# Where tiles begin in the on-chip memory: a pool for small scratch tiles, and other start addresses for weight halves and activations

## The chip, the cores and the metric

The kernel runs on one core of a Trainium2 chip. The core has five engines that run side by side: TensorE (PE in the rows, its weight loads PEld), VectorE (DVE), ScalarE (ACT), GpSimd (POOL) and SyncE (SP), which here issues DMAs. Tiles that the engines read lie in the on-chip memory SBUF, which has 128 partitions; a tile has the same start address, in bytes, on every partition. Matrix products land in another memory, PSUM. The metric is the device time of one execution in microseconds.

## What is computed

Two transformer blocks of depth one run one after the other on 256 tokens of width 2048, all in float32.

```python
# block 1
h = rmsnorm(x, norm_mix_g);  proj = h @ w_in           # 2048 -> 7568 columns
o_a = mla_branch(...);       o_b = dsa_branch(...)     # two kinds of attention
merged = gate0 * (o_a @ w_branch_a) + gate1 * (o_b @ w_branch_b)
x = x + merged @ w_out
x = x + peer_ffn(rmsnorm(x, norm_ffn_g), ...)          # 16384 experts, below
x = rmsnorm(x, norm_final_g)
# block 2: the same frame with an mLSTM and an S5 scan as mixers, then a peer layer and a norm

def peer(x, wq, subkeys, u_tab, v_tab):                # in both blocks
    s = scores(x @ wq, subkeys)                        # two lists of 128 keys per head
    idx, gate = top 16 of the 16 x 16 sums, softmax    # 8 heads x 16 experts per token
    act = gelu(x . u_tab[idx])
    return sum over the 128 chosen of (gate * act) * v_tab[idx]
```

## The kernel before

**Dense experts.** The kernel doesn't gather experts. In each `peer` call it multiplies all 256 tokens with the whole of `u_tab` and, with gates that are zero for experts not chosen, with the whole of `v_tab`. So nearly all of its time goes into matrix products of 256 tokens with weight tiles that come from device memory, 1 MB (128 partitions x 2048 float32) at a time.

**Split operands.** Every such product is made of three matmuls in the format float32r. `weights_now` loads a tile as two halves `w_raw` of 4096 bytes per partition, makes `w_hi` from each on ScalarE (line 198) and `w_lo` = `w_raw` - `w_hi` on VectorE (line 204) or, in part, on GpSimd (line 202). Activations are split in the same way (`split`, lines 252 and 253). `products` (its matmul call is line 213) then issues w_hi x h_hi and w_hi x h_lo in turns, and after them w_lo x h_hi. A matmul has a stationary operand, which is loaded into the array (the LDWEIGHTS rows, 128 columns), and a moving operand, which is streamed through it.

**Three uses of `products`** carry the prediction's steps.

- *u products* (`cols` in `peer`, `in_t`, `gate`, `in_cols`): 128 columns of a weight half are stationary, and 256 columns of `hT_hi` or `hT_lo`, the transposed activations, are moving. PSUM tile `ps_u`. A weight tile makes 48 such matmuls.
- *v products* (`tile_v` in `peer`): 128 columns of the gated activations `coef_hi` or `coef_lo` are stationary, and 512 columns of a weight half are moving. PSUM tile `ps_v`. A weight tile makes 24.
- *row products* (`row_products`, in `rows`, `out_proj`, `lead_products` and for `in2_v`): 128 columns of `hT` are stationary, and 256 to 512 columns of a weight half are moving.

The small ones are those of `mix1` with `cqT`, with `ckvT` and with `o_hi`/`o_lo`, which stand where `hT` stands above.

**Order.** A scheduler of the tile framework sets each engine's order when the program is built. Work for the other engines (routing, gates, attention, scans) is written as generators that `K.step` moves on between weight tiles. Each engine runs its list in order, and semaphores join the lists. The order of `peer` is: queries and routing, then for each half r of the experts one sweep of u products (64 tiles) and one of v products (64 tiles).

**Pools.** A pool is a stretch of SBUF addresses, in which tiles of one tag take turns in `bufs` places. Pools opened on the left stand one behind the other from low addresses, and those with `side="right"` from high ones. Before, the left has const (with `ident`), state (`x` and its squares), weights (`wp`: `w_raw`, `w_hi`, `w_lo`, the `big` tiles, the tags `two_a` and `two_b`, and tiles of a few bytes such as `ss`, `rs_m`, `rs`), and then the pool of the stage at hand; the right has only `top` with `hT`. `two_a` and `two_b` hold `coef_hi` and `coef_lo` among others. Every place is a multiple of 32 bytes.

Of the kernel before, what the change touches and what calls it, by code (L numbers as in the profile page):

```python
# [12 lines left out]
P = 128  # L13
T = 256
TB = 2
# [18 lines left out]
class Ctx:  # L34


    def __init__(self, ctx, tc):
        self.tc, self.nc = tc, tc.nc
        nc = self.nc
        pool = lambda name, bufs, **kw: ctx.enter_context(tc.tile_pool(name=name, bufs=bufs, **kw))  # L40
        self.const = pool("const", 1)
        self.state = pool("state", 1)
        self.top = pool("hT", 1, side="right")
        self.wp = pool("weights", 2)
        self.ps = pool("psum", 2, space=bass.MemoryType.PSUM)
        it = self.const.tile([P, P], F32, name="iota_f")
        nc.gpsimd.iota(it, pattern=[[1, P]], base=0, channel_multiplier=-1,
                       allow_small_or_imprecise_dtypes=True)
        self.diff = it
        self.ident = self.const.tile([P, P], F32, name="ident")  # L50
        nc.vector.tensor_scalar(self.ident, it, 0.0, None, op0=OP.is_equal)
        self.iota = self.const.tile([P, P], F16, name="iota_h")
        nc.gpsimd.iota(self.iota, pattern=[[1, P]], base=0, channel_multiplier=0,
                       allow_small_or_imprecise_dtypes=True)
        self.half_pi = self.const.tile([P, 1], F32, name="half_pi")
        nc.vector.memset(self.half_pi, float(np.pi / 2))
        self.x = self.state.tile([P, TB, D], F32, name="x")
        self.sq = self.state.tile([P, TB, 4], F32, name="x_sq")
        self.sq2 = self.state.tile([P, TB, 4], F32, name="x_sq2")
        self.twice, self.first, self.normed, self.done, self.fused = False, {}, {}, set(), {}  # L60
        self.bg = []
        self.late = []
        self.credit = 0.0
        self.fine = 0
        self.last = None
# [25 lines left out]
            self.square(xx, self.sq[:, tb, c:c + 1])  # L91

    def sum_sq(self, tb, sq):
        ss = self.wp.tile([P, 1], F32, name="ss", bufs=4)
        self.nc.vector.tensor_reduce(ss, sq[:, tb], AX.X, OP.add)
        return ss

# [17 lines left out]
    def norm_begin(self, tb):  # L115

        v = self.nc.vector  # L120
        ss = self.sum_sq(tb, self.sq)
        if self.twice:
            s2 = self.sum_sq(tb, self.sq2)
            e = self.wp.tile([P, 1], F32, name="rs_e", bufs=2)
            v.tensor_scalar(e, ss, EPS / D, EPS * EPS, op0=OP.mult, op1=OP.add)
            rs = self.rsqrt(s2, 1.0 / D, e)
            self.first[tb] = ss
        else:
            rs = self.rsqrt(ss, 1.0 / D)
        for c in range(4):  # L130
            cc = slice(c * 512, (c + 1) * 512)
            n = self.normed_cols(tb, c)
            if (tb, c) in self.fused:
                v.scalar_tensor_tensor(n, self.x[:, tb, cc], rs, self.fused.pop((tb, c)), op0=OP.mult, op1=OP.mult)
            elif (tb, c) not in self.done:
                v.tensor_scalar(n, self.x[:, tb, cc], rs, None, op0=OP.mult)
            elif c % 2:
                self.nc.scalar.activation(n, n, AF.Copy, scale=rs)
            else:
                v.tensor_scalar(n, n, rs, None, op0=OP.mult)  # L140
            self.done.discard((tb, c))
# [95 lines left out]
    def lead_cols(self, src, hh, hl, dst):  # L237

        tiles = [self.weights(src[i], pool=(2048, 1024)[i]) for i in range(2)]
        ps = [self.ps.tile([P, T], F32, name="ps_u", bufs=2) for _ in range(TB)]  # L240
        self.lead_products(ps, tiles, hh, hl, 8, T)
        pt = self.ps.tile([P, 2, T], F32, name="ps_g", bufs=2)
        for tb in range(TB):
            r = self.wp.tile([P, T], F32, name="lead", tag="two_a", bufs=2)
            self.nc.scalar.copy(r, ps[tb])
            for i in range(2):
                self.nc.tensor.transpose(pt[:, i, tb * P:(tb + 1) * P], r[:, i * P:(i + 1) * P], self.ident)
        for i in range(2):
            dst(i, pt[:, i])
# [5 lines left out]
    def rstd(self, src, n, name):  # L255

        nc = self.nc
        junk = self.ps.tile([P, 512], F32, name="ps_u", bufs=2)
        ss = self.wp.tile([P, 1], F32, name=name, tag="rs", bufs=2)
        nc.scalar.activation(junk[:, :n], src, AF.Square, accum_out=ss)  # L260
        return self.rsqrt(ss, 1.0 / n)

    def rsqrt(self, ss, scale, eps=EPS):


        v = self.nc.vector
        m, q, r = (self.wp.tile([P, 1], F32, name=nm, bufs=3) for nm in ("rs_m", "rs_q", "rs_r"))
        v.tensor_scalar(m, ss, scale, eps, op0=OP.mult, op1=OP.add)
        v.tensor_scalar(q.bitcast(I32), m.bitcast(I32), 1, None, op0=OP.logical_shift_right)
        v.tensor_scalar(r.bitcast(I32), q.bitcast(I32), -1.0, float(0x5f3759df), op0=OP.mult, op1=OP.add)  # L270
        v.tensor_scalar(m, m, -0.5, None, op0=OP.mult)
        for _ in range(3):
            v.scalar_tensor_tensor(q, r, m, r, op0=OP.mult, op1=OP.mult)  # L273
            self.last = v.scalar_tensor_tensor(r, q, 1.5, r, op0=OP.add, op1=OP.mult)  # L274
        return r
# [45 lines left out]
def peer(K, wq, keys, u, v, g_out, g_next=None, dst=None, later=None):  # L321
# [8 lines left out]
    nc, ctx = K.nc, ExitStack()  # L330
# [68 lines left out]
    def routing(tb):  # L399
# [23 lines left out]
        nc.vector.tensor_tensor(dif, tv, tv[:, :, 0:1].to_broadcast([P, NH, SEL]), op=OP.subtract)  # L423
        nc.scalar.activation(dif, dif, AF.Exp)
        p_, m1, ms, m3 = new("pos"), new("m1"), new("ms"), new("m3")
        pu, su, au = tv.bitcast(U32), ti, new("au", U32)
        v = nc.vector
        v.tensor_copy(p_, ti)
        v.tensor_scalar(m1, p_, 16.0, None, op0=OP.is_ge)
# [48 lines left out]
    def gates(r, on_pool):  # L478

        def prepare(t0):  # L480
            oh1 = K.wp.tile([P, TG, P], F16, name="oh1", tag="two_a", bufs=2)
            for t in range(TG):
                e = nc.gpsimd if t < on_pool else nc.vector
                e.tensor_scalar(oh1[:, t], K.iota, i1T[:, t0 + t:t0 + t + 1], None, op0=OP.is_equal)  # L484
# [43 lines left out]
    for r in range(2):  # L528
# [29 lines left out]
        for dh in range(2):  # L558
            acc = [[K.ps.tile([P, 512], F32, name="ps_v", bufs=4) for _ in range(2)] for _ in range(TB)]

            def tile_v(jp):
                a = st["A"][jp // 8][:, (2 * jp) % 16:(2 * jp) % 16 + 2]
                ch = K.wp.tile([P, 2, T], F32R, name="coef_hi", tag="two_a", bufs=2)
                cl = K.wp.tile([P, 2, T], F32R, name="coef_lo", tag="two_b", bufs=2)
                K.split(ch, cl, a)
                wh, wl = K.weights(v[dh, r * NJ // 2 + jp])

# [108 lines left out]
def mix1(K, I):  # L676
# [41 lines left out]
    NF = 33  # L718
    inv = wt([NF, 1], "inv", 1)
    nc.gpsimd.dma_start(inv, I["rope_inv"])  # L720
    posi = K.wp.tile([NF, T], I32, name="posi", tag="two_a", bufs=2)
    pap = I["positions"]
    nc.gpsimd.dma_start(posi, bass.AP(tensor=pap.tensor, offset=pap.offset, ap=[[0, NF], [1, T]]))
    gq = K.wp.tile([P, 512], F32, name="gq", tag="two_b", bufs=2)
    nc.gpsimd.dma_start(gq, bass.AP(tensor=I["mla_q_norm_g"].tensor, offset=I["mla_q_norm_g"].offset, ap=[[0, P], [1, 512]]))
    gkv = K.wp.tile([P, 256], F32, name="gkv", tag="two_b", bufs=2)
    nc.gpsimd.dma_start(gkv, bass.AP(tensor=I["mla_kv_norm_g"].tensor, offset=I["mla_kv_norm_g"].offset, ap=[[0, P], [1, 256]]))

    fsel = K.wp.tile([NF, 2, 3, P], F32, name="rope_sel", tag="big", bufs=2)
# [42 lines left out]
    def norm_rows(ps, n, g, dst):  # L772
        nk = n // P
        nms = []
        for tb in range(TB):
            r = K.rstd(ps[tb][:, :n], n, "rs")
            nm = K.wp.tile([P, 512], F32, name="normed", tag="two_a", bufs=2)[:, :n]
            nc.vector.scalar_tensor_tensor(nm, ps[tb][:, :n], r, g, op0=OP.mult, op1=OP.mult)
            nms.append(nm)

# [9 lines left out]
    def rope(dst, ps, kinds):  # L790


        raw = K.wp.tile([P, T], F32, name="rope_raw", tag="two_a", bufs=2)
        nc.scalar.copy(raw, ps)
        m = wt([P, T], "rope_m", 3, tag="one")
        n = 64 if kinds == (1,) else P
# [34 lines left out]
        K.flush()  # L831
        return ps

    both = K.wp.tile([P, T], F32, name="k_both", tag="two_a", bufs=2)
    rope(both, in_t(0), (0, 2))
    for dst, src in ((kpe, 0), (kix, 64)):
        for i in range(2):
# [31 lines left out]
    def attention(dst, scores, V, scale, bias):  # L869

        for hp in range(4):
            pT = wt([P, 2, TB, T], "probsT", 1, tag="four")
            for tb in range(TB):
# [2 lines left out]
                for h in range(2):  # L876
                    scores(S[:, h, :n], 2 * hp + h, tb, n)
                yield 1
                e = K.wp.tile([P, 2, T], F32, name="probs", tag="two_b", bufs=2)
                if bias is None:  # L880
                    m64 = S[:, :, n - 64:n]
                    nc.vector.tensor_tensor(m64, m64, mask[:, 0, None, 64:P].to_broadcast([P, 2, 64]), op=OP.add)
# [321 lines left out]
def mix2(K, I, dram):  # L1204
# [55 lines left out]
    def s5_in(b):  # L1260
# [9 lines left out]
        m1, m2 = wt([P, 2, T], "m1", 2), wt([P, 2, T], "m2", 2)  # L1270
        v.tensor_tensor(m1, px, cb, op=OP.mult)
        v.tensor_tensor(m2, px, sb, op=OP.mult)
        X[b] = xt = K.wp.tile([P, 2, T], F32, name="s5_xt", tag="two_a", bufs=2)
        v.tensor_tensor(xt[:, 0], m1[:, 0], m2[:, 1], op=OP.add)
        v.tensor_tensor(xt[:, 1], m2[:, 0], m1[:, 1], op=OP.subtract)

    def s5_scan(b):
# [4 lines left out]
        for part in range(2):  # L1282
            v.tensor_tensor_scan(st[:, part], mb, xt[:, part], 0.0, op0=OP.mult, op1=OP.add)  # L1283
        m3 = wt([P, 2, T], "m2", 2)
        m4 = K.wp.tile([P, 2, T], F32, name="s5_m4", tag="two_a", bufs=2)
        g.tensor_tensor(m3, st, cb, op=OP.mult)
        v.tensor_tensor(m4, st, sb, op=OP.mult)
        S[b] = m3, m4
# [1 line left out]
    def s5_out(b):  # L1290
        i, q = divmod(b, 4)
        rows = slice(32 * q, 32 * q + 32)
        m3, m4 = S.pop(b)
        s = K.wp.tile([P, 2, T], F32, name="s5_s", tag="two_b", bufs=2)
        g.tensor_tensor(s[:, 0], m3[:, 0], m4[:, 1], op=OP.add)
        g.tensor_tensor(s[:, 1], m3[:, 1], m4[:, 0], op=OP.subtract)
        if q == 0:
            Y[i] = ps_v([P, T])
        return lambda: s5_y(b, s)
# [425 lines left out]
```

## Time and profile before

| | before |
|---|---|
| median of 2 runs | 4360.38 us (4359.77 to 4360.98) |
| the profiled execution, device time | 4360.12 us |
| its span, first to last instruction | 4358.3 us |
| TensorE busy | 4204.3 us, 96% of the span |
| VectorE, ScalarE, GpSimd busy | 3010.1, 2017.6, 1703.3 us |
| TensorE clock granted, mean | 0.987 of the full 2.4 GHz |
| read from device memory | 749.66 MB, 175 GB/s with writes |

The span is the time from the first to the last instruction in the trace; the device time of the same execution is 1.8 us longer. A busy TensorE is one with at least one matmul under way. Matmuls overlap, so the length of one (0.28 us or 0.39 us in the rows) is longer than the distance from its start to the next one's start. The pace of the engine is that distance, and it is read from the start times of the timeline: last start minus first start, divided by the number of matmuls between.

### The profile page before, as it was taken

To read this page: it belongs to the slowest core of one execution; us is meant where nothing else is said; L and a number is where in the kernel's file an instruction comes from. 1 tells how busy PE (TensorE), PEld (TensorE's weight loads), DVE (VectorE), ACT (ScalarE), POOL (GpSimd) and SP (SyncE) were. 2 spreads that over 40 slices of the span, in tenths; PEclk is the share of its full clock that TensorE was granted. 3 is DMA by queue.
4 is the path that set the end of the run, shared out by engine and by line. 5 is a ranking of instruction groups with operands and counts; after the bars stand their busy time and mean duration, and the time that the engine had idled before them with its cause. 6 is when DMAs were issued, how large, how long until landed. Compare 5 with 4: busy or idle time off the path is not lost. (4 is left out here: it accounts for less than half of the span.)

```text
span 4358.3 us, 74041 instructions
## 1 busy us (share of the span) xinstructions
PE 4204.3 (96%) x28929; PEld 3811.5 (87%) x28929; DVE 3010.1 (69%) x4756; ACT 2017.6 (46%) x2847; POOL 1703.3 (39%) x1425
## 2 busy tenths in 40 slices
PE   8999999899999999999988889989999999999999
PEld 7999988899877899988877688989998889999887
DVE  7775569987698566655569976897855555665555
ACT  5565444344444444445543365434444444444454
POOL 1100023886396277500126861368800006771000
PEclk9999999999999999999999999999999999999999
DMA  5445554455666555555656545535555555555554
GB/s 176 159 154 185 184 180 136 141 175 171 208 217 208 184 175 175 175 188 189 205 181 184 160 133 173 166 131 180 172 177 191 186 189 179 175 174 179 189 195 163
DMA packets 220465, 769.19 MB, mean 176 GB/s; under 512 B 25200, under 2 KB 31376, under 8 KB 219217
## 3 DMA queue, kind: packets, MB, share of 16 engines
q1 hardware_dynamic: 214978, 744.79, 51.5%
q0 software_dynamic: 5136, 19.67, 1.2%
q8 instruction: 227, 3.72, 0.3%
q14 instruction: 124, 1.02, 0.1%
HBM read 749.66 MB, written 14.70 MB: 175 GB/s over the span
## 5 line engine op out<-in xcount | busy, mean ns | idle before, releaser
L204 DVE TENSOR_TENSOR w_lo<-w_raw,w_hi 128x1024 fp32r<-128x1024 f32 (+3 forms) x1347 | 1691.4, 1289 | 1175.8 <-issue 918.0
L198 ACT CAST w_hi<-w_raw 128x1024 fp32r<-128x1024 f32 (+1 forms) x1388 | 1445.8, 1045 | 1660.7 <-PE ps_v L213 640.8
L213 PE MATMUL ps_u<-hT_hi,w_hi 128*128 128x256 f32 x5712 | 1419.0, 288 | 16.9 <-DVE gate L1385 10.0
L213 PE MATMUL ps_u<-hT_lo,w_hi 128*128 128x256 f32 x5712 | 1404.5, 285 | 0.0
L484 POOL TENSOR_SCALAR oh<-iota_h,i1T 128x128 f16<-128x128 f16 x896 | 918.3, 1042 | 751.8 <-PE ps_v L213 539.6
L213 PEld LDWEIGHTS ps_u<-hT_hi,w_hi 128*128 128x128 f32 x5712 | 1104.9, 193 | 24.2 <-DVE gate L1385 10.3
L213 PEld LDWEIGHTS ps_u<-hT_lo,w_hi 128*128 128x128 f32 x5712 | 1105.1, 193 | 4.5 <-issue 2.9
L213 PE MATMUL ps_u<-hT_hi,w_lo 128*128 128x256 f32 x5712 | 758.1, 285 | 34.2 <-POOL w_lo L202 18.5
L213 PEld LDWEIGHTS ps_u<-hT_hi,w_lo 128*128 128x128 f32 x5712 | 718.4, 193 | 41.2 <-POOL w_lo L202 19.6
L213 PE MATMUL ps_v<-w_hi,coef_lo 128*128 128x512 f32 x2048 | 698.6, 396 | 6.9 <-DVE coef_lo L253 6.9
L213 PE MATMUL ps_v<-w_hi,coef_hi 128*128 128x512 f32 x2048 | 692.7, 395 | 2.1 <-DVE x L89 2.1
L213 PE MATMUL ps_v<-w_lo,coef_hi 128*128 128x512 f32 x2048 | 525.7, 395 | 0.0
L213 PEld LDWEIGHTS ps_v<-w_hi,coef_lo 128*128 128x128 f32 x2048 | 383.3, 188 | 105.4 <-DVE coef_lo L253 13.3
L213 PEld LDWEIGHTS ps_v<-w_hi,coef_hi 128*128 128x128 f32 x2048 | 384.4, 188 | 96.1 <-ACT coef_hi L252 2.5
L213 PEld LDWEIGHTS ps_v<-w_lo,coef_hi 128*128 128x128 f32 x2048 | 384.4, 188 | 92.6
L202 POOL TENSOR_TENSOR w_lo<-w_raw,w_hi 128x768 fp32r<-128x768 f32 (+3 forms) x159 | 320.9, 2024 | 288.5 <-ACT w_hi L198 132.8
L252 ACT CAST coef_hi<-acts 128x512 fp32r<-128x512 f32 x256 | 158.7, 622 | 189.4 <-PE ps_v L213 186.9
L253 DVE TENSOR_TENSOR coef_lo<-acts,coef_hi 128x512 fp32r<-128x512 f32 x256 | 199.5, 780 | 1.1 <-ACT coef_hi L252 1.0
L112 POOL TENSOR_TENSOR normed<-x,gain 128x512 f32<-128x512 f32 x22 | 37.1, 1709 | 368.2 <-DVE x L89 278.1
L213 PE MATMUL ps_v<-w_hi,hT_hi 128*128 128x512 f32 (+2 forms) x288 | 103.7, 369 | 1.5 <-ACT hT_hi L252 1.5
L213 PE MATMUL ps_v<-w_hi,hT_lo 128*128 128x512 f32 (+2 forms) x288 | 103.3, 367 | 0.7 <-DVE hT_lo L253 0.7
L101 POOL DMA_DIRECT2D gain<-in_final_g x1 | 0.6, 593 | 259.9 <-DVE coef_lo L253 259.9
(469 smaller groups left out, 3785.2 us busy)
## 6 DMA issues: line engine op xcount, KB each, us to landing
w_raw<-in_p_u SPq DMA_DIRECT2D x512, 512.0 KB, 3.9
w_raw<-in_p_v SPq DMA_DIRECT2D x512, 512.0 KB, 3.9
w_raw<-in_in_gates SPq DMA_DIRECT2D x64, 512.0 KB, 4.0
w_raw<-in_w_out SPq DMA_DIRECT2D x64, 512.0 KB, 3.7
w_raw<-in_p_q SPq DMA_DIRECT2D x48, 512.0 KB, 3.8
w_raw<-in_in_t SPq DMA_DIRECT2D x38, 512.0 KB, 4.1
w_raw<-in_w_ab SPq DMA_DIRECT2D x32, 512.0 KB, 4.0
w_raw<-in_in_qk SPq DMA_DIRECT2D x32, 512.0 KB, 3.7
```

Of the source, the lines that this page charges most:

```text
L101: self.nc.gpsimd.dma_start(gb, bass.AP(tensor=g.tensor, offset=g.offset, ap=[[0, P], [1, D]]))
L112: eng.tensor_tensor(self.normed_cols(tb, c), self.x[:, tb, cc], gb[:, cc], op=OP.mult)
L198: nc.scalar.copy(hi[i], raw[i])
L202: nc.gpsimd.tensor_tensor(lo[i][:, m:], raw[i][:, m:], hi[i][:, m:].bitcast(F32), op=OP.subtract)
L204: nc.vector.tensor_tensor(lo[i][:, :m], raw[i][:, :m], hi[i][:, :m].bitcast(F32), op=OP.subtract)
L213: self.last_mm = self.nc.tensor.matmul(out, lhsT=a, rhs=b, start=start, stop=stop)
L252: self.nc.scalar.copy(hi, src)
L253: return self.nc.vector.tensor_tensor(lo, src, hi.bitcast(F32), op=OP.subtract)
L484: e.tensor_scalar(oh1[:, t], K.iota, i1T[:, t0 + t:t0 + t + 1], None, op0=OP.is_equal)
```

## The change

The change moves tiles to other addresses. It opens a pool `small` ahead of `state` for the tiles of a few bytes per partition (`x_sq`, `x_sq2`, `ss`, `rs_e`, `rs`, `rs_m`, `rs_q`, `rs_r`), and a pool `two` behind `weights` for the tags `two_a` and `two_b`. It opens `pad3` on the right outside `hT`, with a tile of 448 bytes that is set to zero once on GpSimd at the start; a second pad has size 0 and no tile. In the routing, `au` no longer has a tile and uses the place of `ms`, which makes 512 bytes of room.

```diff
         self.const = pool("const", 1)
+        self.small = pool("small", 1)
         self.state = pool("state", 1)
+        self.wp = pool("weights", 2)
+        self.pad = pool("pad", 1)
+        self.two = pool("pairs", 2)
+        self.pad3 = pool("pad3", 1, side="right")
         self.top = pool("hT", 1, side="right")
-        self.wp = pool("weights", 2)
+        for p, n in ((self.pad, 0), (self.pad3, 448)):
+            if n:
+                nc.gpsimd.memset(p.tile([P, n // 4], F32, name="pad"), 0.0)
...
-        self.sq = self.state.tile([P, TB, 4], F32, name="x_sq")
+        self.sq = self.small.tile([P, TB, 4], F32, name="x_sq")
...
-        ss = self.wp.tile([P, 1], F32, name="ss", bufs=4)
+        ss = self.small.tile([P, 1], F32, name="ss", bufs=4)
...
-        pu, su, au = tv.bitcast(U32), ti, new("au", U32)
+        pu, su, au = tv.bitcast(U32), ti, ms.bitcast(U32)
...
-                ch = K.wp.tile([P, 2, T], F32R, name="coef_hi", tag="two_a", bufs=2)
-                cl = K.wp.tile([P, 2, T], F32R, name="coef_lo", tag="two_b", bufs=2)
+                ch = K.two.tile([P, 2, T], F32R, name="coef_hi", tag="two_a", bufs=2)
+                cl = K.two.tile([P, 2, T], F32R, name="coef_lo", tag="two_b", bufs=2)
```

The other lines of the diff put the remaining tiles of these names into `small` and `two` in the same way. In the two built programs the instructions of TensorE, ScalarE and SyncE stand in the same order with the same semaphore waits; those of VectorE too, but for the name `ms` in the place of `au`; GpSimd has one more, the zeroing of the pad. What differs is where operands begin. In bytes past a multiple of 512:

| tile | before | after |
|---|---|---|
| `w_raw`, `w_hi`, `w_lo` (every half) | 480 | 0 |
| `coef_hi`, `coef_lo` | 384 | 0 |
| `hT_hi`, `hT_lo` | 480 | 32 |
| `cqT`, `o_hi`, `o_lo` | 0 | 0 |
| `ckvT` | 32 | 32 |
| `k_nope`, `q_nope` | 0 | 0 |
| `kpe` | 160 | 160 |
| `q_pe` | 480 | 0 |

Columns that a matmul takes from these tiles start at further multiples of 512 bytes, but for the 344 and 272 column rows.

On GpSimd the start of the program reads, before:

```order
L1721 UNCONDITIONAL_BRANCH
L47 ISA
L47 IOTA iota_f 128x128
L53 IOTA iota_h 128x128
L720 DMA inv<-in_rope_inv 33x1
```

and after:

```order
L1728 UNCONDITIONAL_BRANCH
L51 MEMSET pad 128x112
L54 ISA
L54 IOTA iota_f 128x128
L60 IOTA iota_h 128x128
L727 DMA inv<-in_rope_inv 33x1
```

The zeroing of the pad stands ahead of the two tables, and nothing else has moved.

## Rows read from the trace of the kernel before

**Rows 1.** The page: engine, busy us (share) xinstructions; granted clock in 40 slices.

```profile
PE 4204.3 (96%) x28929; PEld 3811.5 (87%) x28929; DVE 3010.1 (69%) x4756; ACT 2017.6 (46%) x2847; POOL 1703.3 (39%) x1425
...
PEclk9999999999999999999999999999999999999999
```

**Rows 2.** The page's costliest groups: one of three u groups, of three v groups.

```profile
L213 PE MATMUL ps_u<-hT_hi,w_hi 128*128 128x256 f32 x5712 | 1419.0, 288 | 16.9 <-DVE gate L1385 10.0
...
L213 PE MATMUL ps_v<-w_hi,coef_lo 128*128 128x512 f32 x2048 | 698.6, 396 | 6.9 <-DVE coef_lo L253 6.9
```

**Rows 3.** Timeline of PE, u products: start us, length us, instruction, count.

```profile
1499.79 0.28 PE L213 MATMUL ps_u<-hT_lo,w_hi 128*128 128x256 f32 x1
...
1503.51 2.08 PE L213 MATMUL ps_u<-hT_hi,w_lo 128*128 128x256 f32 x16
```

**Rows 4.** Timeline of PE, v products; eight matmuls from the first row to the second.

```profile
1327.09 0.39 PE L213 MATMUL ps_v<-w_hi,coef_hi 128*128 128x512 f32 x1
...
1328.96 2.02 PE L213 MATMUL ps_v<-w_lo,coef_hi 128*128 128x512 f32 x8
1330.82 1.10 PE L213 MATMUL ps_v<-w_hi,coef_hi 128*128 128x512 f32 x4
```

**Rows 5.** Timeline of PE, row products of out_proj; 24 matmuls between these starts.

```profile
561.27 0.39 PE L213 MATMUL ps_v<-w_hi,hT_hi 128*128 128x512 f32 x1
...
566.71 0.39 PE L213 MATMUL ps_v<-w_hi,hT_hi 128*128 128x512 f32 x1
```

**Rows 6.** Timeline of PE, products with cqT moving; 36 matmuls between these starts.

```profile
90.88 1.10 PE L213 MATMUL ps_u<-cqT,w_hi 128*128 128x256 f32 x8
...
95.12 1.10 PE L213 MATMUL ps_u<-cqT,w_hi 128*128 128x256 f32 x8
```

**Rows 7.** Timeline of PE, products with o_hi moving, and what follows them.

```profile
373.30 1.10 PE L213 MATMUL ps_v<-o_hi,w_lo 128*128 128x256 f32 x8
374.24 0.28 PE L213 MATMUL ps_u<-hT_hi,w_hi 128*128 128x256 f32 x1
```

**Rows 8.** Timeline of PE, ckvT stationary (six matmuls), then ckvT moving (six).

```profile
104.02 0.63 PE L213 MATMUL ps_v<-w_hi,ckvT 128*128 128x512 f32 x2
...
105.42 0.63 PE L213 MATMUL ps_v<-w_hi,ckvT 128*128 128x512 f32 x2
...
106.12 0.63 PE L213 MATMUL ps_u<-ckvT,w_hi 128*128 128x256 f32 x4
...
106.83 0.63 PE L213 MATMUL ps_u<-ckvT,w_hi 128*128 128x256 f32 x4
```

**Rows 9.** Timeline of PE, attention scores in plain float32; four records between.

```profile
209.17 0.60 PE L917 MATMUL ps_v<-k_nope,q_nope 128*128 128x256 f32 x2
209.60 0.59 PE L918 MATMUL ps_v<-kpe,q_pe 128*128 128x256 f32 x2
210.04 0.59 PE L917 MATMUL ps_v<-k_nope,q_nope 128*128 128x256 f32 x2
```

**Rows 10.** Windows: stretch, us, busy us (count) by engine, granted clock, DMA share, GB/s.

```profile
700.00:1100.00 400.00, 372.00 (x3354) 366.76 (x3354) 344.81 (x754) 162.96 (x260) 279.56 (x224) 0.97 0.47 158
1120.00:1480.00 360.00, 350.97 (x1497) 277.97 (x1495) 288.71 (x228) 169.16 (x189) 201.34 (x176) 1.00 0.64 209
1500.00:1870.00 370.00, 370.00 (x3452) 368.62 (x3451) 229.17 (x318) 161.41 (x265) 242.86 (x240) 1.00 0.51 174
3250.00:3600.00 350.00, 350.00 (x1501) 281.56 (x1501) 188.73 (x192) 168.56 (x186) 1.96 (x2) 1.00 0.56 187
```

**Rows 11.** Waits of PE: who waited for whom, us in total, times, longest.

```profile
PE ps_u L213 <- DVE w_lo L204: 18.8, 14, 3.3
...
PE ps_v L213 <- DVE coef_lo L253: 6.9, 14, 0.5
```

**Rows 12.** Timeline of the program's start: GpSimd's first table, and its reader.

```profile
0.83 0.23 POOL L47 IOTA iota_f<- 128x128 f32 x1 [0.40 <-POOLq L1718]
...
2.56 0.15 DVE L51 TENSOR_SCALAR ident<-iota_f 128x128 f32<-128x128 f32 x1
```

More of the change, by code (lines that the diff above doesn't have):

```diff
@@ L57, in __init__ @@
         self.x = self.state.tile([P, TB, D], F32, name="x")
-        self.sq = self.state.tile([P, TB, 4], F32, name="x_sq")
-        self.sq2 = self.state.tile([P, TB, 4], F32, name="x_sq2")
+        self.sq = self.small.tile([P, TB, 4], F32, name="x_sq")
+        self.sq2 = self.small.tile([P, TB, 4], F32, name="x_sq2")
         self.twice, self.first, self.normed, self.done, self.fused = False, {}, {}, set(), {}
@@ L123, in norm_begin @@
             s2 = self.sum_sq(tb, self.sq2)
-            e = self.wp.tile([P, 1], F32, name="rs_e", bufs=2)
+            e = self.small.tile([P, 1], F32, name="rs_e", bufs=2)
             v.tensor_scalar(e, ss, EPS / D, EPS * EPS, op0=OP.mult, op1=OP.add)
@@ L243, in lead_cols @@
         for tb in range(TB):
-            r = self.wp.tile([P, T], F32, name="lead", tag="two_a", bufs=2)
+            r = self.two.tile([P, T], F32, name="lead", tag="two_a", bufs=2)
             self.nc.scalar.copy(r, ps[tb])
@@ L258, in rstd @@
         junk = self.ps.tile([P, 512], F32, name="ps_u", bufs=2)
-        ss = self.wp.tile([P, 1], F32, name=name, tag="rs", bufs=2)
+        ss = self.small.tile([P, 1], F32, name=name, tag="rs", bufs=2)
         nc.scalar.activation(junk[:, :n], src, AF.Square, accum_out=ss)
@@ L266, in rsqrt @@
         v = self.nc.vector
-        m, q, r = (self.wp.tile([P, 1], F32, name=nm, bufs=3) for nm in ("rs_m", "rs_q", "rs_r"))
+        m, q, r = (self.small.tile([P, 1], F32, name=nm, bufs=3) for nm in ("rs_m", "rs_q", "rs_r"))
         v.tensor_scalar(m, ss, scale, eps, op0=OP.mult, op1=OP.add)
@@ L480, in prepare @@
         def prepare(t0):
-            oh1 = K.wp.tile([P, TG, P], F16, name="oh1", tag="two_a", bufs=2)
+            oh1 = K.two.tile([P, TG, P], F16, name="oh1", tag="two_a", bufs=2)
             for t in range(TG):
@@ L720, in mix1 @@
     nc.gpsimd.dma_start(inv, I["rope_inv"])
-    posi = K.wp.tile([NF, T], I32, name="posi", tag="two_a", bufs=2)
+    posi = K.two.tile([NF, T], I32, name="posi", tag="two_a", bufs=2)
     pap = I["positions"]
     nc.gpsimd.dma_start(posi, bass.AP(tensor=pap.tensor, offset=pap.offset, ap=[[0, NF], [1, T]]))
-    gq = K.wp.tile([P, 512], F32, name="gq", tag="two_b", bufs=2)
+    gq = K.two.tile([P, 512], F32, name="gq", tag="two_b", bufs=2)
     nc.gpsimd.dma_start(gq, bass.AP(tensor=I["mla_q_norm_g"].tensor, offset=I["mla_q_norm_g"].offset, ap=[[0, P], [1, 512]]))
-    gkv = K.wp.tile([P, 256], F32, name="gkv", tag="two_b", bufs=2)
+    gkv = K.two.tile([P, 256], F32, name="gkv", tag="two_b", bufs=2)
     nc.gpsimd.dma_start(gkv, bass.AP(tensor=I["mla_kv_norm_g"].tensor, offset=I["mla_kv_norm_g"].offset, ap=[[0, P], [1, 256]]))
@@ L776, in norm_rows @@
             r = K.rstd(ps[tb][:, :n], n, "rs")
-            nm = K.wp.tile([P, 512], F32, name="normed", tag="two_a", bufs=2)[:, :n]
+            nm = K.two.tile([P, 512], F32, name="normed", tag="two_a", bufs=2)[:, :n]
             nc.vector.scalar_tensor_tensor(nm, ps[tb][:, :n], r, g, op0=OP.mult, op1=OP.mult)
@@ L790, in rope @@
     def rope(dst, ps, kinds):
-        raw = K.wp.tile([P, T], F32, name="rope_raw", tag="two_a", bufs=2)
+        raw = K.two.tile([P, T], F32, name="rope_raw", tag="two_a", bufs=2)
         nc.scalar.copy(raw, ps)
@@ L832, in in_t @@
         return ps
-    both = K.wp.tile([P, T], F32, name="k_both", tag="two_a", bufs=2)
+    both = K.two.tile([P, T], F32, name="k_both", tag="two_a", bufs=2)
     rope(both, in_t(0), (0, 2))
@@ L878, in attention @@
                 yield 1
-                e = K.wp.tile([P, 2, T], F32, name="probs", tag="two_b", bufs=2)
+                e = K.two.tile([P, 2, T], F32, name="probs", tag="two_b", bufs=2)
                 if bias is None:
@@ L1272, in s5_in @@
         v.tensor_tensor(m2, px, sb, op=OP.mult)
-        X[b] = xt = K.wp.tile([P, 2, T], F32, name="s5_xt", tag="two_a", bufs=2)
+        X[b] = xt = K.two.tile([P, 2, T], F32, name="s5_xt", tag="two_a", bufs=2)
         v.tensor_tensor(xt[:, 0], m1[:, 0], m2[:, 1], op=OP.add)
@@ L1284, in s5_scan @@
         m3 = wt([P, 2, T], "m2", 2)
-        m4 = K.wp.tile([P, 2, T], F32, name="s5_m4", tag="two_a", bufs=2)
+        m4 = K.two.tile([P, 2, T], F32, name="s5_m4", tag="two_a", bufs=2)
         g.tensor_tensor(m3, st, cb, op=OP.mult)
@@ L1293, in s5_out @@
         m3, m4 = S.pop(b)
-        s = K.wp.tile([P, 2, T], F32, name="s5_s", tag="two_b", bufs=2)
+        s = K.two.tile([P, 2, T], F32, name="s5_s", tag="two_b", bufs=2)
         g.tensor_tensor(s[:, 0], m3[:, 0], m4[:, 1], op=OP.add)
```

## Prediction

> **What bounds the kernel now.** I read the page from the top. TensorE is busy for 4204.3 us of the 4358.3 us span, the next engine, VectorE, for 3010.1 us, and TensorE's granted clock stands at the upper of its two levels, 2.4 GHz, in every slice [rows 1]. The costliest groups are the matmuls of line 213 [rows 2]: three u groups of 5712 (17136 matmuls of 256 columns) and three v groups of 2048 (6144 of 512 columns). In the second half of the sweeps TensorE never idles: 370.00 of 370 us and 350.00 of 350 us [rows 10]. There the end is set by nothing but the pace at which matmuls follow each other, so the question is whether start addresses change this pace.
>
> The pace is read from start times. In the u products 31 matmuls take 1503.51 - 1499.79 = 3.72 us, 120.0 ns each [rows 3]. In the v products 16 take 1330.82 - 1327.09 = 3.73 us, 233.1 ns each [rows 4]. Row products of the same 512 columns take 5.44 us for 24, 226.7 ns each [rows 5]. So 256 more columns cost 226.7 - 120.0 = 106.7 ns, which is one column per tick of 2.4 GHz, and every matmul has a rest beyond its columns: 120.0 - 106.7 = 13.3 ns in u, 226.7 - 213.3 = 13.4 ns in row products, 19.8 ns in v. Times their counts, the rests of u and v are 228 us and 122 us: 350 us is the most that better addresses could give.
>
> The rest isn't constant, and the rows differ in where operands start. In brackets is the distance from the stationary operand's start to the moving one's, modulo 512 bytes, from the table of the section on the change.
>
> - u, moving 480, stationary 480 (0): 120.0 ns.
> - `cqT`, moving 0, stationary 480 (32): 36 in 4.24 us, 117.8 ns [rows 6]; `o_hi`, also 0 and 480 (32): 8 in 0.94 us, 117.5 ns [rows 7].
> - `ckvT`, moving 32, stationary 480 (64): 6 in 0.71 us, 118 ns [rows 8].
> - row products, moving 480, stationary 480 (0): 226.7 ns.
> - v, moving 480, stationary 384 (96): 233.1 ns.
> - `ckvT` stationary at 32, moving 480 (-64): 6 in 1.40 us, 233.3 ns [rows 8].
>
> The same shape costs 2.4 ns or 6.5 ns more or less, at the same clock, with the start as the one difference that I can name.
>
> **The change part by part.** The rows of order say that no instruction moves and no wait is added, so no queue gets longer. Three edits cost nothing. The zeroing of the pad is one GpSimd instruction ahead of a table of 0.23 us, which VectorE reads 1.5 us after it is done [rows 12]; without that slack it would cost about 0.2 us. The shared place of `ms` and `au` is written and read by VectorE alone, in the old order with the old waits. The pools of small tiles change only where a few bytes lie.
>
> *u products, 17136.* After the change the moving operand starts 32 bytes past the stationary one (32 and 0). That distance is the one of `cqT` and `o_hi` before (0 and 480). I take their 117.6 ns: 17136 x 2.4 = 41 us less. From below the bound is a matmul that shows hardly any rest: the attention scores in plain float32, which start at 0 and 0 for half of their records, take 0.87 us for four records, 217.5 ns each [rows 9]; that is twice the 106.7 ns of 256 columns, 213.3 ns, and a rest of 4.2 ns. With it a u matmul would take 110.9 ns, 156 us less in sum. From above: with a moving start of 480, a stationary start of 384 or 32 costs 6.5 ns more than one of 480, and 0 is one more that isn't 480; 17136 x 6.5 = 111 us more.
>
> *v products, 6144.* Moving and stationary start at 0 and 0. The distance 0 has the row products' 226.7 ns as its nearest row, and the start 0 and 0 has the scores' 217.5 ns for as long a stream, in another format. I take the middle, 222 ns: 6144 x 11.1 = 68 us less. The bounds are 217.5 ns (96 us less) and 233.1 ns (no gain). More than 233.1 ns I exclude, since it is the highest pace for 512 columns in the rows.
>
> *Row products with `hT` stationary,* 864 of 512 columns and some 670 shorter. The distance goes from 0 to -32, between 226.7 ns (0) and 233.3 ns (-64). I take half: 1534 x 3.3 = 5 us more, with bounds of 14 us less (the scores' rest) and 10 us more.
>
> *Small ones.* `cqT` and `o_hi`, 912 matmuls, go from distance 32 to 0, thus from 117.6 to 120 ns: 2 us more.
>
> *What is late next.* Where other engines already make TensorE wait, part of the gain is lost. In the first u sweep TensorE is busy 372 of 400 us beside a VectorE at 345, and in the first v sweep 351 of 360 us [rows 10]; the waits there are for `w_lo` and `coef_lo` of VectorE [rows 11]. Those stretches would gain 3354 x 2.4 = 8 us and 1497 x 11.1 = 17 us, and the same in block 2 less clearly; I let 7 us go. Data flow at 175 GB/s on average and at 209 in the fastest of these stretches, so a pace 2% higher asks for nothing new of the DMAs.
>
> The sum is -41 - 68 + 5 + 2 + 7 = -95 us. The profiled execution took 4360.1 us, 0.3 us under the median, with 1.8 us of it outside the span. **4360 - 95 = 4265 us.**
>
> **The rivals.**
>
> *Nearly the whole rest goes.* If the rest comes from operands that start off a 512-byte boundary, and a weight tile at 0 frees both kinds of product, u reaches 111 ns and v 217.5 ns: -156 - 96 - 14 us, and some 15 us lost to the engines of rows 11, gives 4109 us. Half of that is 4235 us, so the case spans 4100 to 4225 us. For it speaks that plain float32 at 0 and 0 has a rest of 4 ns; against it that the scores with other starts, the `kpe` row of rows 9 (160 and 480), keep the same pace, so that their small rest may come from the format.
>
> *Starts don't matter in steps of 32 bytes.* The differences of 2.4 and 6.5 ns would then come from what stands around those products, such as the PSUM tile or the work of other engines, and the time stays at 4350 to 4368 us. Against it: rows 4 and 5 differ by 6.4 ns with the same count of columns and the same target in PSUM, and v keeps its pace in sweeps with much and with little GpSimd work [rows 10].
> The Trainium skill's page "SBUF — State Buffer" (Specifications) gives cache lines of 16 bytes and a cost for each new line; all starts here, old and new, are multiples of 32 bytes, so by that rule nothing changes and this rival's time holds. Rows 6 and 3 disagree: 117.8 against 120.0 ns with the same number of such lines. The Trainium skill's page "TensorE: Matmul & The Clock Gate" (Step-by-step) says that weight loads have a read port of their own and take nothing from the running matmul; by that rule the stationary start can't matter, and of v only the step of the moving start from 480 to 0 would be left. Rows 4 and 5 disagree, 233.1 against 226.7 ns at the same moving start.
>
> *Only v gains.* If the distance rule doesn't carry over to other absolute starts, u may stay at 120 ns, and v at 226.7 ns gives 39 us: 4321 us. It is the forecast with its smaller half of support.
>
> *Slower.* If what counts is the stationary start alone, and 480 is the one good start in the rows while 384 and 32 cost 6.5 ns, then a weight tile at 0 costs each u matmul 6.5 ns, and v, with its stationary start at 0 instead of 384, gains nothing: +111 + 10 + 6, 4487 us. It decides from u at 122.5 ns on, where the loss in u equals what v gains at 226.7 ns. Against it: with the stationary start fixed at 480, the moving start still makes 2.4 ns, so that the pair counts and not one of them. For it: no row shows float32r with a stationary start of 0.
>
> **How the numbers follow.** Forecast 0.42, within 4225 to 4300 us; nearly the whole rest 0.27; only v 0.10; no effect 0.11; slower 0.10. A change of under 2%, 87 us, can't be told from none by a measurement of this kernel, so faster means under 4273 us. The forecast stands astride of it and gives 0.23 to faster and 0.19 to no change; with the rivals that makes 0.50 faster, 0.40 the same, 0.10 slower. The range leaves out the slower case (0.10) and the lower part of the case of the whole rest (under 0.10): 4120 to 4366 us.
>
> **What would show it.** In timelines of the changed kernel, in the sweeps without waits: u at 117.6 ns (16 matmuls of `w_lo` from start to the next group in 1.88 us instead of 1.92), v at 222 ns (eight in 1.78 us instead of 1.86), row products of 512 columns at 230 ns, `o_hi` at 120 ns. The distance rule is wrong if u and `o_hi` don't trade places. The prediction as a whole is wrong if u falls under 115 ns or rises over 122 ns, since each nanosecond there is 17 us, or if TensorE's new idle time is more than some 15 us.

## The result and the profile after

The changed kernel takes **4300.43 us** (median of 2 runs, 4297.87 to 4302.99), the kernel before 4360.38 us (4359.77 to 4360.98). That is 60 us or 1.4% less, a ratio of 0.986 with a 95% interval of 0.982 to 0.991: a real gain, and smaller than the 2% from which the prediction speaks of faster. The profiled execution of the changed kernel took 4302.99 us, against 4360.12 us before: 57 us less.

The page of the changed kernel: span, busy us (share) by engine, granted clock in 40 slices.

```profile
span 4301.2 us, 74042 instructions
...
PE 4127.4 (96%) x28929; PEld 3767.9 (88%) x28929; DVE 3018.2 (70%) x4756; ACT 2016.2 (47%) x2847; POOL 1716.8 (40%) x1426
...
PEclk9999999999999999999999999999999999999999
```

Against [rows 1] the counts are the same but for the zeroing on GpSimd, the mean granted clock is 0.985 instead of 0.987, and TensorE is still the busiest engine by far. Its busy time fell by 4204.3 - 4127.4 = 77 us, the span by 57 us. So TensorE idles about 20 us more than before. The line numbers of all instructions are 7 higher.

The timeline of TensorE in the changed kernel, a u sweep: start us, length us, instruction, count.

```profile
1499.78 0.28 PE L220 MATMUL ps_u<-hT_lo,w_hi 128*128 128x256 f32 x1
...
1502.93 2.03 PE L220 MATMUL ps_u<-hT_hi,w_lo 128*128 128x256 f32 x16
1504.80 0.20 PE L505 MATMUL ps_g<-rh,oh 128*128 128x64 f16 x1
```

27 matmuls lie between the first two starts: 3.15 us, 116.7 ns each, where [rows 3] had 120.0. The sixteen with `w_lo` take 1.87 us to the next group, 116.9 ns each.

The same view in a v sweep.

```profile
1324.69 0.39 PE L220 MATMUL ps_v<-w_hi,coef_hi 128*128 128x512 f32 x1
...
1326.51 1.98 PE L220 MATMUL ps_v<-w_lo,coef_hi 128*128 128x512 f32 x8
1328.32 1.07 PE L220 MATMUL ps_v<-w_hi,coef_hi 128*128 128x512 f32 x4
1330.01 1.20 PE L220 MATMUL ps_v<-w_hi,coef_lo 128*128 128x512 f32 x4 [0.62 <-DVE coef_lo L260]
```

Sixteen matmuls take 1328.32 - 1324.69 = 3.63 us, 226.9 ns each, against 233.1 in [rows 4]. The last row shows the other side: TensorE now runs ahead and waits 0.62 us for `coef_lo`.

The same view in out_proj (row products, 24 matmuls between the first two starts), and with `o_hi` moving.

```profile
565.09 0.40 PE L220 MATMUL ps_v<-w_hi,hT_hi 128*128 128x512 f32 x1
...
570.69 0.40 PE L220 MATMUL ps_v<-w_hi,hT_hi 128*128 128x512 f32 x1
...
370.75 1.12 PE L220 MATMUL ps_v<-o_hi,w_lo 128*128 128x256 f32 x8
371.71 0.28 PE L220 MATMUL ps_u<-hT_hi,w_hi 128*128 128x256 f32 x1
```

These two kinds lost. 24 row products take 5.60 us, 233.3 ns each, against 226.7 in [rows 5], and `o_hi` takes 0.96 us for 8, 120 ns, against 117.5 in [rows 7]. u and `o_hi` have traded places.

Windows of the changed kernel in the stretches that answer to [rows 10], and then its waits of PE.

```profile
700.00:1100.00 400.00, 365.26 (x3355) 359.79 (x3354) 342.25 (x753) 162.88 (x260) 285.29 (x224) 0.96 0.48 159
1115.00:1475.00 360.00, 343.84 (x1492) 276.46 (x1491) 296.76 (x227) 168.08 (x188) 200.88 (x176) 1.00 0.64 209
1495.00:1860.00 365.00, 365.00 (x3488) 363.69 (x3487) 230.74 (x319) 163.21 (x267) 245.77 (x243) 1.00 0.54 180
3225.00:3560.00 335.00, 335.00 (x1479) 277.39 (x1479) 184.10 (x189) 168.53 (x185) 0.00 (x0) 1.00 0.58 194
```

```profile
PE ps_u L220 <- POOL w_lo L209: 24.5, 6, 10.7
...
PE ps_u L220 <- DVE w_lo L211: 20.1, 13, 3.2
PE ps_v L1312 <- POOL s_s L1302: 18.7, 13, 3.4
PE ps_v L220 <- DVE coef_lo L260: 14.5, 24, 0.6
```

In the last two stretches TensorE is still busy all of the time and starts 9.56 matmuls per us instead of 9.33 (3488 in 365 us, 3452 in 370), and 4.41 instead of 4.29.

In the first two, the first u sweep and the first v sweep of block 1, the gain is gone. The count in 400 us hasn't moved (3354 before, 3355 after) while busy time fell from 372.00 to 365.26 us, and in 360 us it is 1492 after 1497. The second u sweep begins at nearly the same time, before and after:

```profile
1488.17 0.28 PE L213 MATMUL ps_u<-hT_hi,w_hi 128*128 128x256 f32 x1
...
1487.99 0.28 PE L220 MATMUL ps_u<-hT_hi,w_hi 128*128 128x256 f32 x1
```

So all but 0.2 us of the 57 come from what follows. In the first u sweep TensorE waits for `w_lo`, and more of it for GpSimd's part than for VectorE's. Its waits from 700 to 1100 us, before and after:

```profile
PE ps_u L213 <- POOL w_lo L202: 11.0, 3, 7.7
PE ps_u L213 <- DVE w_lo L204: 9.7, 8, 2.7
...
PE ps_u L220 <- POOL w_lo L209: 15.8, 4, 10.7
PE ps_u L220 <- DVE w_lo L211: 10.4, 9, 3.2
```

The longest, 7.7 us and then 10.7, is for a `w_lo` that stands on GpSimd behind 18 to 19 us of `oh` tiles, and it ends at 787.3 us before and 786.2 after: TensorE only comes to it earlier. In the first v sweep the wait for `coef_lo` doubled, from 14 times and 6.9 us [rows 11] to 23 times and 14.0 us, nearly all of the 24 times and 14.5 us above; and ScalarE's `w_hi` waited longer for the weights to arrive, before and after:

```profile
ACT w_hi L198 <- DMA w_raw<-in_p_v: 15.1, 9, 2.2
...
ACT w_hi L205 <- DMA w_raw<-in_p_v: 28.1, 17, 2.7
```

What sets the length of that sweep wasn't separated.

### The profile page after: what moved, and what is told of

The parts are those of the page before. It is cut to its first block, busy times and chain, and to the rows that moved or that the text cites. A ratio compares the mean times of both kernels' runs of the same rounds, so it can differ in the third digit from the quotient of the medians.

```text
span 4301.2 us, 74042 instructions
## 1 busy us (share of the span) xinstructions
PE 4127.4 (96%) x28929; PEld 3767.9 (88%) x28929; DVE 3018.2 (70%) x4756; ACT 2016.2 (47%) x2847; POOL 1716.8 (40%) x1426
## 5 line engine op out<-in xcount | busy, mean ns | idle before, releaser
L220 PE MATMUL ps_u<-hT_hi,w_hi 128*128 128x256 f32 x5712 | 1390.1, 285 | 16.4 <-DVE gate L1392 10.0
L220 PE MATMUL ps_u<-hT_lo,w_hi 128*128 128x256 f32 x5712 | 1374.5, 282 | 0.0
L491 POOL TENSOR_SCALAR oh<-iota_h,i1T 128x128 f16<-128x128 f16 x896 | 932.2, 1058 | 707.5 <-PE ps_v L220 529.8
L220 PEld LDWEIGHTS ps_u<-hT_hi,w_hi 128*128 128x128 f32 x5712 | 1086.9, 190 | 23.7 <-DVE gate L1392 10.3
L220 PEld LDWEIGHTS ps_u<-hT_lo,w_hi 128*128 128x128 f32 x5712 | 1086.8, 190 | 4.0 <-issue 2.3
L220 PE MATMUL ps_u<-hT_hi,w_lo 128*128 128x256 f32 x5712 | 739.1, 281 | 41.4 <-POOL w_lo L209 24.5
L220 PEld LDWEIGHTS ps_u<-hT_hi,w_lo 128*128 128x128 f32 x5712 | 699.1, 189 | 47.3 <-POOL w_lo L209 25.5
L220 PE MATMUL ps_v<-w_hi,coef_lo 128*128 128x512 f32 x2048 | 687.1, 391 | 14.5 <-DVE coef_lo L260 14.5
L220 PE MATMUL ps_v<-w_lo,coef_hi 128*128 128x512 f32 x2048 | 512.0, 389 | 0.0
L498 DVE TENSOR_TENSOR rh<-oh,g_hi 128x512 f16<-128x512 f16 x128 | 101.3, 791 | 0.9 <-PE ps_g L506 0.9
```

The lines of the kernel that those rows point to most:

```text
L220: self.last_mm = self.nc.tensor.matmul(out, lhsT=a, rhs=b, start=start, stop=stop)
L498: nc.vector.tensor_tensor(rh, oh2, b2(gh), op=OP.mult)
```

## The experiments

**The question.** The pace changed, but by which rule? Three theories were set against each other.

- *Distance*: only the moving start minus the stationary start counts.
- *Absolute starts*: a weight tile or `coef` on a multiple of 512 is what is good.
- *Regrouping*: the pool of small tiles does it, whatever the starts.

All eleven kernels are the changed kernel with three pads, which shift `coef`, the weights and `hT` against each other. They compute the same, and the instructions of all engines stand in the order of the changed kernel, but for the zeroing of pads. The edit, as it reads for the first:

```diff
-        self.wp = pool("weights", 2)
-        self.pad = pool("pad", 1)
+        self.pad0 = pool("pad0", 1)
         self.two = pool("pairs", 2)
+        self.pad = pool("pad", 1)
+        self.wp = pool("weights", 2)
...
-        for p, n in ((self.pad, 0), (self.pad3, 448)):
+        for p, n in ((self.pad0, 0), (self.pad, 0), (self.pad3, 480)):
```

The others differ from it in that last line alone. Paces below are the mean distance between consecutive starts of matmuls of a kind over the whole trace, leaving out distances over 1.25 times the median (these are waits). By that measure the kernel before has 119.8 ns in u, 233.3 in v, 227.1 in row products, and the changed kernel 116.9, 226.9 and 233.3.

**All three at 0**

> Weight halves, coef and hT all start at multiples of 512 bytes; against the changed kernel only hT moves, from 32 to 0. Theory (the distance from the stationary to the moving start sets the pace): u products go back to 120.0 ns, v products stay at 226.7 ns, row products with hT stationary return to 226.7 ns from 233; the time is about 4300 + 53 - 6 = 4347 us. Rival (multiples of 512 bytes are what helps): u stays at 117 ns or falls below it, time 4295 us or less. Rival (the stationary start alone counts, 0 being a good one): u stays at 117 ns, row products change, 4295 to 4300 us.

Measured: 4333.0 us (4 runs, 4331.32 to 4334.22; before 4359.97 in 7 runs beside it), ratio 0.994 (0.992 to 0.995). u at 119.8 ns, v at 226.9, row products at 227.2. Its timeline in the u sweep:

```profile
1499.75 0.28 PE L221 MATMUL ps_u<-hT_hi,w_hi 128*128 128x256 f32 x1
...
1503.59 0.28 PE L221 MATMUL ps_u<-hT_hi,w_hi 128*128 128x256 f32 x1
```

32 in 3.84 us, 120.0 ns. u has distance 0 again, and the pace of before, with every start at 0: the start itself gives u nothing. The time is 14 us lower than the 4347 us that I had for it. The paces came out; what I had not counted is that fewer waits grow when only v is faster: the time of u beyond its steady pace is 81.8 us here and 87.7 in the changed kernel.

**All three shifted by 224**

```diff
-        for p, n in ((self.pad0, 0), (self.pad, 0), (self.pad3, 480)):
+        for p, n in ((self.pad0, 224), (self.pad, 0), (self.pad3, 224)):
```

> All of the changed kernel's tiles in question are shifted by 224 bytes: weights and coef start at 224, hT at 256, modulo 512; all distances are those of the changed kernel. Theory (distance): u 117 ns, v 226.7 ns, row products 233 ns, o products 120 ns, all as in the changed kernel, time 4290 to 4310 us. Rivals (multiples of 512 bytes, or the stationary or the moving start alone): at least one of these paces moves by 2 ns or more, and the time by 35 us or more.

Measured: 4296.89 us (4 runs, 4293.04 to 4298.42), ratio 0.985 (0.984 to 0.987). Its timeline in the u sweep:

```profile
1484.72 2.03 PE L221 MATMUL ps_u<-hT_hi,w_lo 128*128 128x256 f32 x16
1486.59 0.28 PE L221 MATMUL ps_u<-hT_hi,w_hi 128*128 128x256 f32 x1
```

1.87 us for 16, 116.9 ns; v stands at 226.8 and row products at 233.2. With `coef` and weights at 224 and `hT` at 256, none of these three starts is where it was, and every pace and the time are those of the changed kernel. Absolute starts fall as the cause.

**v at the distance of before, then at 32**

```diff
-        for p, n in ((self.pad0, 0), (self.pad, 0), (self.pad3, 480)):
+        for p, n in ((self.pad0, 0), (self.pad, 96), (self.pad3, 352)):
```

> One part undone: weights start 96 bytes past coef as in the kernel before (coef 0, weights 96), and hT stays 32 bytes past the weights (128). Theory (distance): v goes back to 233.1 ns, u stays at 117 ns, time about 4300 + 6144 x 6.4 ns = 4339 us. Rival (the stationary start alone): v, whose stationary start is 0 as in the changed kernel, stays at 226.7 ns, and u, whose stationary start moves from 0 to 96, changes. Rival (multiples of 512): both get slower.

```diff
-        for p, n in ((self.pad0, 0), (self.pad, 0), (self.pad3, 480)):
+        for p, n in ((self.pad0, 0), (self.pad, 32), (self.pad3, 416)):
```

> Coef starts at 0, weights 32 bytes past it, hT 32 bytes past the weights (64). Theory (distance): u stays at 117 ns; v has the distance at which the 256-column products are 3 ns faster than at distance 0, so 223.7 ns if 512 columns behave alike, time about 4300 - 18 = 4282 us. If 512 columns have another best distance, v is at 226.7 ns or above. Rival (stationary start alone, 0 in v): v stays at 226.7 ns, time about 4300 us.

Measured: 4333.22 us (4 runs, 4332.28 to 4339.17), ratio 0.994 (0.993 to 0.996), and 4334.81 us (4 runs, 4331.03 to 4339.28), ratio 0.994 (0.993 to 0.996). In both u is at 117.1 ns and v at 233.3. The v sweep of the second:

```profile
1322.67 0.39 PE L221 MATMUL ps_v<-w_hi,coef_hi 128*128 128x512 f32 x1
...
1324.54 2.03 PE L221 MATMUL ps_v<-w_lo,coef_hi 128*128 128x512 f32 x8
1326.41 1.10 PE L221 MATMUL ps_v<-w_hi,coef_hi 128*128 128x512 f32 x4
```

16 in 3.74 us, 233.8 ns. The first was as the distance theory says: distance 96 brings back the v pace of before. The second missed its first guess. I had carried the gain of distance 32 in u (256 columns) over to v (512 columns) and expected 223.7 ns; the distance that is good for 256 columns is bad for 512. So each shape has a table of its own, and the next runs measured it.

**Other distances: 64, 128, 192 and 256**

```diff
-        for p, n in ((self.pad0, 0), (self.pad, 0), (self.pad3, 480)):
+        for p, n in ((self.pad0, 0), (self.pad, 64), (self.pad3, 352)):
```

> Weights start 64 bytes past coef, hT 64 bytes past the weights (0, 64, 128). Theory (only the distance counts): u as ckvT did before at 64, 118 ns; v somewhere from 226.9 to 233.3 ns, and at 233.3 ns if for 512 columns the distance 0 alone is good; about 4340 us then. Rival (multiples of 64 bytes are what help, since 0 was good for v and 32 and 96 were not): v stays at 226.9 ns, about 4310 us.

```diff
-        for p, n in ((self.pad0, 0), (self.pad, 0), (self.pad3, 480)):
+        for p, n in ((self.pad0, 0), (self.pad, 128), (self.pad3, 224)):
```

> Coef 0, weights 128, hT 256. If the pattern repeats every 128 bytes, this is distance 0 again: u 119.8 ns, v 226.9 ns, 4333 us as with all tiles at 0. If it doesn't, v is at 233.3 ns, and u is open between 117 and 120 ns.

```diff
-        for p, n in ((self.pad0, 0), (self.pad, 0), (self.pad3, 480)):
+        for p, n in ((self.pad0, 0), (self.pad, 256), (self.pad3, 32)):
```

> Coef 0, weights 256, hT 448: v at distance 256, u at 192. If the pattern repeats every 128 or 256 bytes, v is at 226.9 ns; if the distance must be 0 modulo 512, at 233.3 ns. u at 192: as at 64 (118 ns) with a period of 128 bytes.

```diff
-        for p, n in ((self.pad0, 0), (self.pad, 0), (self.pad3, 480)):
+        for p, n in ((self.pad0, 0), (self.pad, 192), (self.pad3, 32)):
```

> Coef 0, weights 192, hT 448: v at distance 192, u at 256. With a period of 256 bytes u is as at 0, 119.8 ns; v as at -64, 233.3 ns. A pace under 116 ns in u or under 226 ns in v at any distance of these four would mean that the changed kernel's distances aren't the best ones.

Measured, one run each beside one of the kernel before at 4363.32 us: 4317.46 (u 117.7, v 228.9), 4353.24 (u 118.9, v 232.5), 4262.61 (u 114.5, v 226.8) and 4367.94 us (u 119.9, v 233.3). The v sweep of the third, distance 256:

```profile
1301.65 1.98 PE L221 MATMUL ps_v<-w_lo,coef_hi 128*128 128x512 f32 x8
1303.47 1.07 PE L221 MATMUL ps_v<-w_hi,coef_hi 128*128 128x512 f32 x4
```

1.82 us for 8, 227.5 ns, within rounding the pace of distance 0. In the fourth it is u that has distance 256, and it keeps the 119.9 ns of distance 0. So 256 reads as 0 in both shapes, and 128 doesn't. The first came out 22 us below the 4340 us that I had for it, because v at distance 64 is one of the better places; with 228.9 ns there and 232.5 at 128, multiples of 64 alone aren't what helps. The fourth also answers the regrouping theory: it has the new pools and the zeroing, but no good distance, and its time is near that of the kernel before (4367.94 against 4363.32 us). The third gave something not looked for, u at 114.5 ns.

**Distances 96 and 160**

```diff
-        for p, n in ((self.pad0, 0), (self.pad, 0), (self.pad3, 480)):
+        for p, n in ((self.pad0, 0), (self.pad, 160), (self.pad3, 224)):
```

> Coef 0, weights 160, hT 256. Theory (the distance modulo 256 bytes sets the pace): row products with hT stationary, at -96, which is 160 modulo 256, and v at 160 have the same pace per 512 columns, between 226.9 and 233.3 ns; u at 96 has not been seen yet, 114 to 120 ns. Rival (the period is 512 bytes): row products and v differ.

```diff
-        for p, n in ((self.pad0, 0), (self.pad, 0), (self.pad3, 480)):
+        for p, n in ((self.pad0, 0), (self.pad, 0), (self.pad3, 320)):
```

> Coef and weights 0, hT 160. Theory (distance modulo 256): v at 226.9 ns; row products of 512 columns at -160, which is 96, at 233.3 ns as v was at 96; u at 160 not seen yet, 114 to 120 ns. If u is under 114.5 ns, this is the best kernel so far, if not, the one with hT at 192.

Measured, one run each (before 4360.87 us in 9 runs beside them): 4376.43 us, with u at 119.9 and v at 234.3 ns, and 4317.06 us, with u at 118.4 and v at 226.8. The first is the slowest of all, 16 us over the kernel before. Its v sweep:

```profile
1301.09 2.04 PE L221 MATMUL ps_v<-w_lo,coef_hi 128*128 128x512 f32 x8
1302.97 1.09 PE L221 MATMUL ps_v<-w_hi,coef_hi 128*128 128x512 f32 x4
```

1.88 us for 8, 235 ns. Row products at -96, which is 160 modulo 256, take 234.3 ns here as v does, and in the second kernel at -160, which is 96, 233.4 ns as v did at 96 (233.3): the period is 256 bytes. An arrangement with a good look to it (`coef` at 0, weights at 160, `hT` at 256) can thus cost time.

**The best of each: u at 192, v at 0**

```diff
-        for p, n in ((self.pad0, 0), (self.pad, 0), (self.pad3, 480)):
+        for p, n in ((self.pad0, 0), (self.pad, 0), (self.pad3, 288)):
```

> Coef and weights 0, hT 192: the changed kernel with another distance in u alone. Theory (distance modulo 256): u 114.5 ns as with weights at 256 and hT at 448, v 226.9 ns, row products 229 ns at -192, which is 64; 17136 x 2.4 = 41 us less than the changed kernel and 864 x 4.3 = 4 us less: 4255 to 4265 us. Rival (the absolute starts of 256 and 448 made that kernel fast): u stays near 117 ns and the time near 4297 us.

Measured: **4259.72 us** (5 runs, 4256.19 to 4262.64), ratio 0.977 against the kernel before (0.975 to 0.978). It beats both kernels: 101 us under the kernel before, and some 41 us under the changed one. Its page, and its u sweep:

```profile
span 4258.5 us, 74042 instructions
...
PE 4082.0 (96%) x28929; PEld 3725.6 (87%) x28929; DVE 3013.7 (71%) x4756; ACT 2018.1 (47%) x2847; POOL 1713.3 (40%) x1426
...
1491.80 0.28 PE L221 MATMUL ps_u<-hT_lo,w_hi 128*128 128x256 f32 x1
...
1494.63 1.98 PE L221 MATMUL ps_u<-hT_hi,w_lo 128*128 128x256 f32 x16
1496.45 0.28 PE L221 MATMUL ps_u<-hT_hi,w_hi 128*128 128x256 f32 x1
```

41 matmuls take 4.65 us, 113.4 ns each (114.3 over the whole trace). v stands at 226.9 and row products at 229.0. With weights at 256 and `hT` at 448 u had 114.5 ns: again the distance of 192 decides, and not the starts.

**The table that these runs make.** Distance is the moving start minus the stationary one, modulo 256 bytes; paces in ns. Runs that share a distance agree within 0.2 ns, and the table has one of them; empty cells weren't measured.

| distance | 256 columns, u | 256 columns, rows | 512 columns, v | 512 columns, rows |
|---|---|---|---|---|
| 0 | 119.8 | 119.8 | 226.9 | 227.1 |
| 32 | 116.9 | | 233.3 | |
| 64 | 117.7 | 116.9 | 228.9 | 229.0 |
| 96 | 119.9 | 119.8 | 233.3 | 233.4 |
| 128 | 118.9 | 118.8 | 232.5 | 232.4 |
| 160 | 118.4 | 118.2 | 234.3 | 234.3 |
| 192 | 114.3 | 115.3 | 233.3 | 233.3 |
| 224 | | 118.2 | | 233.3 |

"Rows" are row products, where the operands change sides: `hT` is stationary, the weights are moving, and the distance has the opposite sign. For 512 columns both kinds agree within 0.2 ns at each distance, though other tiles, other starts and other work stand around them. For 256 columns they agree as well but for 64 and 192, where they lie 0.8 and 1.0 ns apart; why is open.

## Why the prediction was right

**The step that carried it holds.** The prediction took the distance between the two starts as the variable, and gave u the pace of `cqT` and `o_hi` at the same distance before [rows 6, 7]. u came out at 116.9 ns, and u and `o_hi` traded places as it asked. What it got wrong in that rule is its period, 256 bytes and not 512.

**The terms of the sum**, predicted and measured:

- u: 41 us less predicted, 17136 x (119.8 - 116.9) = 50 us less measured in the steady pace.
- v: 68 us less predicted, 6144 x (233.3 - 226.9) = 39 us less measured. **This is the mis-sized term.** The prediction took 222 ns as the middle between the row products' 226.7 ns at the same distance [rows 5] and the plain float32 scores' 217.5 [rows 9]. The row of the same format was right to 0.2 ns; the row of another format had nothing to say, and its weight cost 30 us.
- Row products: 5 us more predicted, as half way between two paces for 1534 matmuls (the trace has 1632, with 768 shorter ones instead of 670). Measured, the 864 of 512 columns went the whole way (6.2 ns, 5.4 us more), and the 384 of 256 columns gained 1.6 ns each (0.6 us): 5 us more, right in the sum and not in its parts.
- `cqT` and `o`: 2 us more predicted, 2 us measured in the steady pace.
- Lost to waits: 7 us predicted. In u the time over the steady pace grew by 8 us (79.8 to 87.7), in v by 11 us (13.4 to 24.0), in `cqT` by 3 us, and in row products it fell by 2 us: 20 us. **This is the second mis-sized term**, 13 us too small. The prediction laid the waits on VectorE; the larger part of them in the first u sweep was, and is, for GpSimd's `w_lo`. It also gave the two first sweeps 8 + 17 us of gain less 7, where the runs show 0.2 us up to the end of both, and it asked nothing new of the DMAs, where ScalarE's wait for weights grew from 15.1 to 28.1 us.

Measured terms: -50 - 39 + 5 + 2 + 20 = -62 us, against 57 us between the two profiled executions; the rest, waits in the S5 scan among it (for `s_s`, 13.9 to 18.7 us), isn't broken down further. The v term 29 us too large and the loss 13 us too small, against a u term 9 us too small, make 33 of the 35 us between the predicted 4265 us and the measured 4300.43.

**What was luck.** The stated range, 4120 to 4366 us, also holds the time of no change, so that a time within it says little; the paces are what bears the mechanism out. The forecast's own band, 4225 to 4300 us, was missed by 0.4 us, and one of the prediction's signs of being wrong came true: TensorE's idle time grew by 20 us, more than the 15 it allowed. The errors of u and of v partly cancelled.

**The clock** reads too well in the prediction. The digit 9 of [rows 1] means 90% or more, and in the clock's records TensorE is at the lower level, 1.2 GHz, for 116 us of the kernel before and 127 of the changed one. It isn't the reason for the loss: in both kernels about 200 u matmuls follow each other in these stretches, 213 ns apart.

**The rivals.** *Nearly the whole rest goes* is out: no distance that was tried brought v under 226.8 ns or u under 114.3, and plain float32's small rest didn't carry over. *Starts don't matter in steps of 32 bytes* is out by the first two runs: 4333.0 and 4296.89 us differ by nothing but the place of `hT` and the common shift. The Trainium skill's page "SBUF — State Buffer" (Specifications), with cache lines of 16 bytes, would have these two alike; the runs disagree, 119.8 against 116.9 ns in u with all starts on multiples of 32 bytes. *Only v gains* (4321 us) lies 21 us from the time, but its cause is refuted: u gained 50 us, more than v. *Slower, by the stationary start alone* is out: with the stationary `coef` at 0 in both, v took 226.9 ns with the moving weights at 0 and 233.3 at 32, and with the stationary weights at 0 in both, u took 119.8 ns with `hT` at 0 and 116.9 at 32.

**Where the gain goes.** Of what the steady paces give, about three quarters arrive. By the table, u, v and the 512-column rows together would save 84 us in the changed kernel and 132 us in the best one; 60 and 101 us arrived. The first sweeps of block 1 show where much of the rest goes: TensorE waits for GpSimd and VectorE in the u sweep, and the v sweep takes 373.1 us from its first start to its last before and 373.7 after, at 233.4 and 227.4 ns, where the other three go from 358 us to 348 or 349.

**What stays open** is the mechanism. That a stationary operand is loaded while the operand before it still streams, and that the two reads collide or not according to their distance, fits the table; it was only argued, since no row shows a read. Nor is it known why 192 is the best place for 256 columns and among the worst for 512. Distances that aren't multiples of 32 weren't tried.

## What to carry to other kernels

When TensorE is busy nearly all of the time and still spends more than its columns per matmul, compare the paces of the same shape between places that differ in start addresses, and treat the distance of moving and stationary start as a tuning knob to be swept per shape: here a few hundred bytes of pad were worth 101 us in 4361. Size such a term from rows of the same format and shape alone, and ask stretch by stretch who else sets its length: in the changed kernel two sweeps of eight gave next to nothing. A start that looks clean (all at 0) isn't the best one.

## What was not expected of the hardware

- The pace depends on the distance of two starts, modulo 256 bytes, and not on the starts: a common shift by 224 bytes left u, v and row products within 0.1 ns.
- The range is wide for so small a cause: 114.3 to 119.9 ns for 256 columns, 226.8 to 234.3 ns for 512, at the same granted clock.
- The two shapes want different distances: 192 gives the best pace of 256 columns and one of the worst of 512 (233.3), and 0 gives the best of 512 and one of the worst of 256 (119.8).
